# Holding back a kernel's second load until VectorE has built the identity matrix

## The chip, the cores and the metric

The kernel runs on one core of one Trainium2 chip. The metric is the time of one execution in microseconds (us) on the device, as the median of several executions. A second figure is used below, the *span*: the time from the first to the last instruction in the trace, which is about 1.8 us shorter than the time of the execution.

Some words are used throughout. An *issue* is the instruction with which SyncE starts a load. The load is then carried out by 16 DMA engines in pieces; the trace has one *record* for each piece, and a record of the first three loads is the 60 KB that go into one partition. A *descriptor* is the entry that tells a DMA engine to move one piece. A load has *landed* when its last record is in.

## The reference

```python
batch, seq, dim = 32, 512, 1024          # float32
def reference(x):
    return np.max(x, axis=-1).astype(np.float32)
```

16384 rows of 1024 numbers are reduced to 16384 maxima. 67.1 MB are read, 64 KB are written.

## The kernel before

The input goes through a ring of 46 rows in each of the 128 partitions. SyncE issues the loads, VectorE reduces each load with `reduce_max`. The first three loads have 15 rows each and fill 45 of the 46 places, so the fourth load cannot be issued until the first has been reduced. For a small part of the rows near the end TensorE, ScalarE and GpSimd take over a piece of the reduction, and for that VectorE builds an identity matrix at the start. The parts that matter here:

```python
    in_turn("DVE", nc.vector.memset(ident, 1.0))
    ...                                     # iota by scan, transpose, three small adds
    in_turn("DVE", nc.vector.tensor_scalar(
        out=ident, in0=colno, scalar1=rowno[:, 0:1], scalar2=None, op0=ALU.is_equal))
    ...
    for j in range(len(loads)):
        while issued < len(loads) and issued < j + 3:
            start, n, src, _ = loads[issued]
            held = any(s < start + n and start < s + k for s, k, _, _ in loads[j:issued])
            if held:                        # the place in the ring is still in use
                break
            nc.sync.dma_start(out=rows(issued), in_=src)
            issued += 1
        ...
            maximum(res[:, col:col + n - m], rows(j)[:, :n - m, :])
```

## Time and profile before

| | before |
|---|---|
| time, median of 5 | 164.09 us (163.90 to 164.27) |
| span of the profiled run | 162.3 us |
| share of the span in which the loads' queue is busy | 96.7% |
| VectorE busy | 135.4 us, 83% |
| issues of the first three loads | 0.72, 1.14, 1.62 us |
| VectorE ends the identity | 2.50 us |
| first reduction starts | 21.42 us |

The table is read like this. Two resources are near full, the 16 DMA engines and VectorE. About three quarters of VectorE's missing 17% (19.9 of 26.9 us) lie before the first reduction, because it has no data yet. The lines for this stand in the prediction.

### The profile page before, as it was taken

How to read it: one execution, taken by the hardware profiler on the slowest of the kernel's cores; microseconds unless marked ns; L12 is line 12 of the kernel's file. 1: busy time of each engine (PE TensorE's matmuls, PEld its weight loads, DVE VectorE, ACT ScalarE, POOL GpSimd, SP SyncE). 2: the span in 40 equal slices, each digit the busy share in tenths (PEclk: the TensorE clock that was granted, in tenths of full speed). 3: DMA queues.
4: the chain of work that ended last, by engine and by line, in shares of the span. 5: the costliest groups of instructions: out<-in, count | busy, mean ns of one | idle time of the engine just before them, and what ended most of it. 6: DMA issues, size and time to landing. Idle time of an engine off the chain costs nothing.

```text
span 162.3 us, 305 instructions
## 1 busy us (share of the span) xinstructions
PE 14.0 (9%) x76; PEld 12.0 (7%) x76; DVE 135.4 (83%) x35; ACT 6.3 (4%) x8; POOL 16.2 (10%) x11
## 2 busy tenths in 40 slices
PE   0000000000000000000000000000003010736540
PEld 0000000000000000000000000000002010725440
DVE  3000079995999779998999999999999999999994
ACT  3000000000000000000000000000001000222020
POOL 0000000000000000000000000000000500095970
DMA  7999699988999699999998998999999999999990
GB/s 242 485 485 454 273 485 485 485 379 348 485 485 485 285 410 452 452 452 388 497 472 371 433 455 355 436 436 420 509 396 445 452 395 396 440 411 423 405 379 18
DMA packets 3200, 67.18 MB, mean 414 GB/s; under 512 B 640, under 2 KB 640, under 8 KB 1408
## 3 DMA queue, kind: packets, MB, share of 16 engines
q1 hardware_dynamic: 2880, 67.11, 96.7%
q10 hardware_dynamic: 320, 0.07, 0.2%
HBM read 67.11 MB, written 0.07 MB: 414 GB/s over the span
## 4 chain that ended last, share of the span: by engine, by line
DVE 57%; DMA 36%; issue 5%; DVEq 0%
DVE res L168 52%; DMA ring<-in_x_dram 36%; DVE fetched L168 5%; DVEq L249 0%
## 5 line engine op out<-in xcount | busy, mean ns | idle before, releaser
L168 DVE TENSOR_REDUCE res<-ring 128x15 f32<-128x15360 f32 (+10 forms) x15 | 124.1, 8302 | 23.7 <-DMA ring<-in_x_dram 23.7
L143 POOL PARTITION_ALL_REDUCE top<-sb x7 | 16.0, 2330 | 141.8 <-ACT sb L141 141.8
L135 PE MATMUL ps<-ident,ring 128*128 128x128 f32 x38 | 9.3, 425 | 133.8 <-DMA ring<-in_x_dram 133.8
L135 PEld LDWEIGHTS ps<-ident,ring 128*128 128x128 f32 x38 | 7.5, 223 | 134.1 <-issue 127.8
L141 ACT COPY sb<-ps 128x768 f32<-128x768 f32 (+3 forms) x7 | 5.1, 739 | 150.2 <-PE ps L135 150.2
L168 DVE TENSOR_REDUCE fetched<-ring 128x2 f32<-128x1280 f32 (+3 forms) x5 | 8.5, 1699 | 0.0
L161 PE MATMUL fetched<-ident,top 1*128 1x1 f32 x38 | 4.8, 243 | 10.8 <-DVE fetched L168 7.3
L161 PEld LDWEIGHTS fetched<-ident,top 1*128 1x128 f32 x38 | 4.5, 213 | 12.5 <-issue 8.0
L168 DVE TENSOR_REDUCE res<-res 128x2 f32<-128x672 f32 (+1 forms) x2 | 1.7, 858 | 0.0
L141 ACT ACT_TABLE_LOAD x1 | 1.3, 1283 | 0.7 <-PEq L238 0.7
L83 DVE MEMSET ident<- 128x128 f32 x1 | 0.2, 165 | 0.8 <-PEq L238 0.8
L168 DVE TENSOR_REDUCE res<-fetched 128x2 f32<-128x8 f32 (+3 forms) x5 | 0.7, 158 | 0.0
L90 DVE TENSOR_SCALAR rowno<-rowno 32x1 f32<-32x1 f32 x3 | 0.4, 146 | 0.1
L85 DVE TENSOR_TENSOR_SCAN colno<-ident 128x128 f32<-128x128 f32 x1 | 0.4, 425 | 0.0
L92 DVE TENSOR_SCALAR ident<-colno,rowno 128x128 f32<-128x128 f32 x1 | 0.3, 285 | 0.0
L87 DVE STREAM_TRANSPOSE rowno<-colno 128x32 f32<-128x32 f32 x1 | 0.2, 213 | 0.0
L238 POOL MEMSET const-float32-0.0<- 128x1 f32 x1 | 0.1, 98 | 0.2 <-issue 0.2
L238 POOL MEMSET const-bfloat16-1.0<- 128x1 bf16 x1 | 0.1, 101 | 0.0
L238 POOL MEMSET const-uint8-127<- 128x1 uint8 x1 | 0.1, 101 | 0.0
L238 POOL MEMSET const-float32-1.0<- 128x1 f32 x1 | 0.1, 99 | 0.0
L84 DVE MEMSET rowno<- 128x32 f32 x1 | 0.1, 85 | 0.0
## 6 DMA issues: line engine op xcount, KB each, us to landing
ring<-in_x_dram SPq DMA_DIRECT2D x3, 7680.0 KB, 38.4
ring<-in_x_dram SPq DMA_DIRECT2D x1, 7168.0 KB, 37.0
ring<-in_x_dram SPq DMA_DIRECT2D x1, 6144.0 KB, 33.4
ring<-in_x_dram SPq DMA_DIRECT2D x1, 5632.0 KB, 28.6
ring<-in_x_dram SPq DMA_DIRECT2D x1, 4608.0 KB, 39.1
ring<-in_x_dram SPq DMA_DIRECT2D x1, 4096.0 KB, 33.3
ring<-in_x_dram SPq DMA_DIRECT2D x1, 3584.0 KB, 29.0
ring<-in_x_dram SPq DMA_DIRECT2D x1, 3072.0 KB, 35.9
```

What stands on the lines that cost most here:

```text
L83: in_turn("DVE", nc.vector.memset(ident, 1.0))
L84: in_turn("DVE", nc.vector.memset(rowno, 0.0))
L85: in_turn("DVE", nc.vector.tensor_tensor_scan(out=colno, data0=ident, data1=ident, initial=-1.0, op0=ALU.add, op1=ALU.mult))
L87: in_turn("DVE", nc.vector.transpose(out=rowno, in_=colno[:, :32]))
L90: in_turn("DVE", nc.vector.tensor_scalar(out=part, in0=part, scalar1=float(q * 32), scalar2=None, op0=ALU.add))
L92: in_turn("DVE", nc.vector.tensor_scalar(out=ident, in0=colno, scalar1=rowno[:, 0:1], scalar2=None, op0=ALU.is_equal))
L135: in_turn("PE", nc.tensor.transpose(out=ps[:, k * P:(k + 1) * P], in_=rows(j)[:, loads[j][1] - m + r + i, c0 * P:(c0 + 1) * P], identity=i ...
L141: in_turn("ACT", nc.scalar.copy(out=sb[:, :W], in_=ps[:, :W]))
L143: in_turn("POOL", nc.gpsimd.partition_all_reduce(top[:, :W], sb[:, :W], P, bass_isa.ReduceOp.max))
L161: in_turn("PE", nc.tensor.transpose(out=share(j)[:, c0, r + i:r + i + 1], in_=tops[j, c][0:1, k * P:(k + 1) * P], identity=ident[0:1, 0:1],))
L168: return in_turn("DVE", nc.vector.reduce_max(out=out, in_=in_, axis=X))
L238: nc = _bacc.Bacc("TRN2", target_bir_lowering=False, num_devices=1)
```

## The change

The intent, by the reason that the new line gives, is "first load alone": nothing else is to be issued while the first load starts.

```diff
-    in_turn("DVE", nc.vector.tensor_scalar(
+    ready = in_turn("DVE", nc.vector.tensor_scalar(
         out=ident, in0=colno, scalar1=rowno[:, 0:1], scalar2=None, op0=ALU.is_equal))
 ...
-            nc.sync.dma_start(out=rows(issued), in_=src)
+            load = nc.sync.dma_start(out=rows(issued), in_=src)
+            if issued == 1:
+                tc.add_manual_dep(load.ins, ready.ins.name, SYNC, reason="first load alone")
             issued += 1
```

## The prediction

> **What bounds the kernel now.** I read the page first (busy shares, then the DMA row of the forty slices), then the chain that ended last in order of time, then the waits of VectorE and of the loads' queue, then the first three microseconds of the timeline, and last the single DMA records of the trace.
>
> The page's busy line and DMA rows say that two things are nearly full, VectorE at 83% and the 16 DMA engines from the first slice to the last but one:
>
> ```profile
> PE 14.0 (9%) x76; PEld 12.0 (7%) x76; DVE 135.4 (83%) x35; ACT 6.3 (4%) x8; POOL 16.2 (10%) x11
> DMA  7999699988999699999998998999999999999990
> q1 hardware_dynamic: 2880, 67.11, 96.7%
> ```
>
> The loads' queue (q1) is busy for 96.7% of the 162.3 us span, 156.9 us. The dips to 6 in the slices are an effect of how long records are put into slices: each record of a large load covers one row group of 60 KB and takes 2.27 us, and in the records each engine takes the next one up in the same moment that it ends the last, with nothing longer than 0.06 us between, apart from single records that the trace seems to lack. 67.11 MB over 16 engines at 61440 bytes in 2.267 us (27.1 GB/s each, 434 together) is 154.8 us. The transfers begin at 1.72 us and end near 158.5 us, so their own start, about 155 us of data and a couple of microseconds of small losses are the whole span.
>
> The chain in order of time says the same for the first half, and shows where VectorE takes over:
>
> ```profile
> 0.66 0.07 issue
> 0.72 20.67 DMA ring<-in_x_dram
> 21.39 0.02 issue
> 21.42 16.16 DVE res L168
> 37.58 0.02 issue
> 37.60 37.02 DMA ring<-in_x_dram
> 74.62 0.02 issue
> 74.64 55.86 DVE res L168 x5
> ```
>
> The reader should see that the 37.02 us of the fourth load, issued at 37.60, are not its own transfer (7.34 MB at 434 GB/s is 16.9 us): it lies behind the third load in the queue. So up to 74.62 the clock is the stream of data, whatever the chain names. After 74.64 VectorE's reductions run end to end (the only other idle time it has is before that):
>
> ```profile
> DVE res L168 <- DMA ring<-in_x_dram: 23.7, 4, 18.9
> ```
>
> Those four waits are 18.91 us before the first reduction, 1.98 and 1.99 before the next two, 0.79 before the fourth. Hence everything later hangs on when the fourth load lands, and that on when the stream started and how fast it went.
>
> The start itself:
>
> ```profile
> 0.72 1.32 SPq L185 DMA_DIRECT2D ring<-in_x_dram  x3
> 0.82 0.17 DVE L83 MEMSET ident<- 128x128 f32 x1 [0.82 <-PEq L238]
> 0.94 0.09 DVE L84 MEMSET rowno<- 128x32 f32 x1
> 1.02 0.42 DVE L85 TENSOR_TENSOR_SCAN colno<-ident 128x128 f32<-128x128 f32 x1
> 1.48 0.21 DVE L87 STREAM_TRANSPOSE rowno<-colno 128x32 f32<-128x32 f32 x1
> 1.72 0.46 DVE L90 TENSOR_SCALAR rowno<-rowno 32x1 f32<-32x1 f32 x3
> 2.22 0.28 DVE L92 TENSOR_SCALAR ident<-colno,rowno 128x128 f32<-128x128 f32 x1
> ```
>
> Three loads are issued from 0.72 to 2.04 us: in single records the first takes 372 ns, the second starts at 1.14 and takes 425, the third starts at 1.62 and takes 424. VectorE finishes the identity at 2.22 + 0.28 = 2.50 us.
>
> **What the Trainium skill says.** "DMA: Bandwidth & Descriptors", section "Queues, rings and completion order", says that on each engine descriptors are consumed in ring order. The trace agrees: all sixteen engines do eight 2.27 us records of the first load before any of the second (the second load's first records start at 20.5 us). So the second load does not share bandwidth with the first now, and a "first load alone" gets no bandwidth back that way. The page "Perfetto Trace Analysis", section "DMA Instruction — HWDGE (DVE, Sync)", says the recorded span of an issue is the wait for and use of the descriptor generator, not the movement of data, and that an engine may begin while descriptors are still being made. The trace agrees: issues of 0.33 to 0.45 us stand for transfers of 16 us. "VectorE: DVE Perf Modes", section "The perf-mode tier table (the rule you actually need)", has tensor_reduce at 1x only; 15360 elements in 16.15 us is 0.951 elements per ns, so the reductions have no slack that a change in load timing could reach.
>
> **The change part by part.**
>
> Added: one wait on the second issue. It moves from 1.14 to about 2.50 + 0.05 = 2.55 us (0.05 from the 0.04 to 0.07 us between other VectorE ends and the dependent step in this timeline), the third from 1.62 to about 3.03 us. Late by 1.4 us, and it costs nothing: the engines need the second load's descriptors only when the first load's are used up, at 20.5 us, 17.5 us after the third issue. No instruction is removed, and the order on every engine stays the same; the built kernels show that only SyncE gets a split issue and a wait. The first load, the activation table and VectorE's steps are untouched.
>
> What could be gained lies in the first records. The sixteen first ones start between 1.72 and 2.52 us and take 3.0 us where they start early, against 2.267 us for every later one; the two that start last (2.44 and 2.52) take 2.27 and 2.33. All end together, between 4.68 and 4.94, but for one engine at 5.20. It is as if nothing moved at full speed before about 2.45 us, 1.7 us after the issue. That is when the third issue is through (2.04) plus some delay, so the descriptors of the second and third loads may be holding up the rest of the first load's. If so:
> - if the early starters lose their stretch but the last still starts at 2.52, the first round ends at 4.85 instead of 5.20: gain 0.35 us;
> - if all start with their neighbours, the slowest (start 2.02, took 3.17) ends at 2.02 + 2.27 = 4.29: gain 0.9 us;
> - if the stretch is a cold start that has nothing to do with the other issues: gain 0.
>
> Against the first two: the issue at 37.60, made in mid-stream, lengthened the records then in flight by at most 0.01 us (2.267 to 2.279). One more issue costs the engines almost nothing once they run. So I give no effect about half, and the gains the other half at some 0.55 us on average: -0.3 us.
>
> A gain at the start is passed on in full. The first landing moves the first reduction, which frees the slot for the fourth load; the stream is continuous, so landings two to four move as much; VectorE from 74.64 on has no idle time, and its later loads' issues hang on its own ends, so they move along too. Sum: 163.97 - 0.3 = 163.65 us.
>
> **The rivals.**
> 1. *Nothing at all.* The wait is hidden behind 17.5 us of queued data and the slow first records are a cold start. For it: the small cost of issues in mid-stream. It makes 163.9 to 164.0.
> 2. *The whole start-up stretch goes.* For it: the second and third issues take 425 ns where a lone one takes 328, so issues do crowd each other, and the end of the stretch falls just after the third. It makes 163.1, or 162.9 if the last engine also stops trailing the rest by 0.25 us, which it does through the first four landings.
> 3. *The late issue makes a hole in the stream.* It would need the first load's data to run out by 3 us; they last to 20.5. Against it the whole timeline; it would make more than 164 only if the queue behaved in another way than ring order.
> 4. *The engines' order shifts.* The stagger of the sixteen engines is set in the first round and kept for the whole kernel; another stagger may put one engine later, as one now is by 0.25 us. That is worth 0.2 us either way.
>
> **Range and chances.** The three runs of before lie within 163.9 and 164.27, so noise is 0.2 us. The largest plausible gain is 0.9 us, the largest plausible loss the stagger and noise, 0.4 us. The range is 163.0 to 164.2. A 2% change is 3.3 us, over three times the largest gain that I can build from the records and far over any loss; both sides get 1%.
>
> **What would show it.** In the changed profile, the second and third issues should stand at about 2.55 and 3.0 us; the sixteen first records should take about 2.3 to 2.7 us if the crowding is real, or still end at 4.7 to 5.2 us if not; the first reduction should start at 21.42 minus the gain (20.5 to 21.4), the fourth at 74.64 minus the same, and the time from the fourth to the end should not move. The second reduction's wait should stay at 1.98 us. I would be wrong if the first reduction moved one way and the end another, if VectorE waited for the second load by more than 2.2 us, or if the end moved by over 1 us: then something later in the stream depends on the early issues in a way that these views do not show.

## More of the kernel before

One view that it does not show is what SyncE, the issuer of the loads, waits for. In these lines of the kernel before, the columns are the waiting line, what it waited for, the total in us, how often, and the longest:

```profile
SPq L185 <- DVE res L168: 86.3, 6, 16.2
SPq L185 <- DMA ring<-in_x_dram: 37.6, 5, 19.4
...
SPq L238 <- PEq L238: 0.7, 1, 0.7
```

SyncE spends most of the kernel waiting, and the longest single wait is the 19.4 us from the third issue to the landing of the first load.

## The result, and the profile after

The changed kernel took 164.11 us (median of 5, 163.97 to 164.18), the kernel before 164.09 us (median of 5, 163.90 to 164.27). The ratio is 1.0003, with a 95% interval of 0.9991 to 1.0015. Ratios here are the mean time of one kernel's fast runs over that of the other's of the same rounds, so they are not quite the ratio of the medians quoted. The result is: no change.

The wait did go where it was meant to go. The first line below is from the timeline of the first microseconds of the changed kernel (start, duration, engine, instruction, count), the second the end of the identity:

```profile
0.72 2.63 SPq L185 DMA_DIRECT2D ring<-in_x_dram  x3
2.22 0.29 DVE L92 TENSOR_SCALAR ident<-colno,rowno 128x128 f32<-128x128 f32 x1
```

Three issues that took from 0.72 to 2.04 us now take until 3.35 us; the second stands at 2.54 and the third at 2.92. In the view of what SyncE waits for, with the columns as above, the new wait has a line of its own, and another line has shrunk:

```profile
SPq L185 <- DVE res L168: 86.3, 6, 16.2
SPq L185 <- DMA ring<-in_x_dram: 36.2, 5, 18.0
...
SPq L185 <- DVE ident L92: 1.4, 1, 1.4
```

The wait is 1.4 us long. The wait that follows it on the same engine, for the first landing, went from 19.4 to 18.0 us: the same 1.4 us less. This is what an absorbed wait looks like in a profile. It is not gone, it is taken out of a longer wait behind it.

The busy shares and the DMA rows of the page:

```profile
PE 14.0 (9%) x76; PEld 12.0 (7%) x76; DVE 135.4 (83%) x35; ACT 6.3 (4%) x8; POOL 16.2 (10%) x11
DMA  7997999979999599999998998999999999999991
q1 hardware_dynamic: 2880, 67.11, 96.8%
```

The chain that ended last, its first eight pieces (start, duration, what), and VectorE's waits for loads:

```profile
0.66 0.07 issue
0.72 20.62 DMA ring<-in_x_dram
21.34 0.02 issue
21.37 16.16 DVE res L168
37.53 0.02 issue
37.55 37.00 DMA ring<-in_x_dram
74.55 0.02 issue
74.57 55.86 DVE res L168 x5
```

```profile
DVE res L168 <- DMA ring<-in_x_dram: 23.6, 4, 18.9
```

The first reduction starts at 21.37 us in place of 21.42, the fourth at 74.57 in place of 74.64. These shifts of 0.05 and 0.07 us are a little larger than those between two executions of the changed kernel (21.37 and 21.39, then 74.57 and 74.61), and well under the 0.2 us of noise that the prediction allowed. From the fourth reduction's start to the end of the span it is 87.7 us in both kernels, and VectorE's waits are the same four. The second reduction, before and then after:

```profile
39.55 16.15 DVE L168 TENSOR_REDUCE res<-ring 128x15 f32<-128x15360 f32 x1 [1.98 <-DMA ring<-in_x_dram]
39.48 16.15 DVE L168 TENSOR_REDUCE res<-ring 128x15 f32<-128x15360 f32 x1 [1.96 <-DMA ring<-in_x_dram]
```

The figure in brackets is the idle time before it. The prediction wanted this wait to stay at 1.98 us.

### The profile page after: what moved, and what is told of

Its sections match the earlier page's. It is cut to its first block, busy times and chain, and to the rows that moved or that the text cites. A ratio compares the mean times of both kernels' runs of the same rounds, so it can differ in the third digit from the quotient of the medians.

```text
span 162.2 us, 305 instructions
## 1 busy us (share of the span) xinstructions
PE 14.0 (9%) x76; PEld 12.0 (7%) x76; DVE 135.4 (83%) x35; ACT 6.3 (4%) x8; POOL 16.2 (10%) x11
## 4 chain that ended last, share of the span: by engine, by line
DVE 57%; DMA 36%; issue 5%; DVEq 0%
DVE res L168 52%; DMA ring<-in_x_dram 36%; DVE fetched L168 5%; DVEq L251 0%
```

## The experiments

The result alone leaves something open. The prediction gave even chances to a gain of 0.35 to 0.9 us, which would come from first DMA records that are no longer slowed by the second and third issues. The measured zero can mean that there was no such slowing, or that the second issue, now at 2.54 us, slows the same records at another moment. I also wanted to see how much later the second issue may come, and whether a shift of the start reaches the end at all.

The table shows the sixteen first records of a stream of transfers, as the trace of each run has them. The kept trace doesn't name the engine of a record; that there is one for each engine is inferred from the order of starts and ends. A record of this size takes 2.267 us in mid-stream. Each run is told below.

```
                issues of the loads    first records start   mean length   they end
before          0.72, 1.14, 1.62       1.72 to 2.52          2.89 us       4.68 to 5.20
changed         0.72, 2.54, 2.92       1.72 to 2.63          3.03          4.71 to 5.14
after_again     0.72, 2.54, 2.92       1.72 to 2.42          2.98          4.71 to 5.17
late_10         0.73, 12.68, 13.06     1.73 to 2.52          2.94          4.57 to 5.05
first_waits     2.53, 2.95, 3.43       3.54 to 4.30          2.93          6.37 to 6.90
landed, load 2  21.38 (load 3: 21.76)  22.35 to 22.97        2.97          25.18 to 25.77
```

### after_again: the changed kernel once more

No edit.

> The changed kernel once more, unedited, five rounds. Theory A (the wait is hidden behind the 17 us of the first load's data, and the slow first records are a cold start): ratio to the kernel before 0.999 to 1.001, the first reduction starting within 0.1 us of 21.4 us, sixteen first records of about 2.3 to 3.3 us again. Theory B (the descriptors of the second load do slow the first records, a gain of 0.3 us that noise covered): ratio 0.998, first reduction at 21.1 us or before.

Measured: 164.06 us (median of 5) against 164.04 us; ratio 1.000, interval 0.9988 to 1.0013. The first reduction starts at 21.39 us. These are theory A's numbers, and theory B's hidden gain of 0.3 us (0.2%) is outside the interval. That the slow records are a cold start, this run doesn't test.

### late_10: the same wait, ten microseconds longer

```diff
+    for _ in range(6):
+        ready = in_turn("DVE", nc.vector.memset(res, 0.0))
```

These lines stand after the identity in the changed kernel. The area that is cleared is written again later, and the results are correct.

> The wait of the change, only longer: six clears of a scratch area follow the identity on VectorE, and the second load waits for the last, at an estimated 8 to 12 us. Theory A: 164.0 us, no change, because the first load's data last to 20.5 us; its sixteen first records still take about 3 us. Theory B (in the changed kernel the second issue, at 2.54 us, merely falls on the first records at another point and slows them as much): now nothing is issued while they run, so they take 2.27 us, the first reduction starts 0.35 to 0.9 us before 21.4, and the time is 163.1 to 163.6 us. Theory C (a late second issue costs as it stands): longer by up to the delay, 5 to 10 us.

Measured: 164.02 us (median of 4) against 164.04 us; ratio 0.9998, interval 0.9985 to 1.0012. The issues of the first three loads, and the first reduction:

```profile
0.73 12.75 SPq L187 DMA_DIRECT2D ring<-in_x_dram  x3
21.36 16.15 DVE L170 TENSOR_REDUCE res<-ring 128x15 f32<-128x15360 f32 x1 [8.71 <-DMA ring<-in_x_dram]
```

The second issue stands at 12.68 us, over 7 us after the last first record has ended, and the first records are as slow as ever: 2.94 us on average. So theory B falls. The descriptors of other loads are not what slows the first records, since here there were none. Whether the making of the first load's own descriptors does, this run leaves open. Theory C falls too: eleven and a half microseconds of delay cost nothing.

### landed: the second load waits until the first is there

```diff
-            nc.sync.dma_start(out=rows(issued), in_=src)
+            load = in_turn("SP", nc.sync.dma_start(out=rows(issued), in_=src))
+            if issued == 0:
+                lead = load
             if issued == 1:
-                tc.add_manual_dep(load.ins, ready.ins.name, SYNC, reason="first load alone")
+                tc.add_manual_dep(load.ins, lead.ins.name, SYNC, reason="first load landed")
```

The edit is to the changed kernel. The loads at the end are put into the same order on SyncE, so that no later load can be moved ahead of the one that waits.

> The second load waits until the first has landed, so it is issued at about 21.4 us, after the data have run out at 20.5 to 21.0 us. Theory A: a hole in the stream from 20.8 us to the second load's first record, 1.0 us after the issue, so about 22.4 us: landings two to four and the end later by 1.6 us, 165.6 us, and by 2.3 us, 166.3 us, if the engines' first records after the hole are again 0.7 us too long. Rival (VectorE idles about 2 us before the second and third reductions, so there is slack): under 0.3 us.

Measured: 166.57 us (median of 4) against 164.04 us, 2.5 us longer; ratio 1.0153, interval 1.0139 to 1.0167. The timeline (start, duration, what, then in brackets the idle time before and what ended it) of VectorE, and after the dots the fourth reduction of the kernel before:

```profile
21.39 16.15 DVE L168 TENSOR_REDUCE res<-ring 128x15 f32<-128x15360 f32 x1 [18.88 <-DMA ring<-in_x_dram]
41.97 16.15 DVE L168 TENSOR_REDUCE res<-ring 128x15 f32<-128x15360 f32 x1 [4.42 <-DMA ring<-in_x_dram]
60.11 16.16 DVE L168 TENSOR_REDUCE res<-ring 128x15 f32<-128x15360 f32 x1 [1.99 <-DMA ring<-in_x_dram]
77.06 15.09 DVE L168 TENSOR_REDUCE res<-ring 128x14 f32<-128x14336 f32 x1 [0.80 <-DMA ring<-in_x_dram]
...
74.64 15.09 DVE L168 TENSOR_REDUCE res<-ring 128x14 f32<-128x14336 f32 x1 [0.79 <-DMA ring<-in_x_dram]
```

The wait before the second reduction grew from 1.98 to 4.42 us, by 2.44 us, and it is not made good anywhere: the fourth reduction starts at 77.06 in place of 74.64 us, and the execution takes 2.5 us longer. Idle time of VectorE in front of a load is no slack if the stream of data is what sets the end. The loss has the two parts expected. The engines stand still from 20.5 to 21.0 us, when each runs out, to 22.35 to 22.97 us, about 1.8 us; and their first records after the pause are again 0.7 us too long, at a time when nothing of the kernel's launch is left. So the slow start comes with starting the stream, and not with the start of the program.

### first_waits: the wait on the first load instead

```diff
-            if issued == 1:
+            if issued == 0:
                 tc.add_manual_dep(load.ins, ready.ins.name, SYNC, reason="first load alone")
```

As in landed, the order of SyncE's loads is fixed.

> The wait for the identity is put on the first load instead of the second, so the first issue moves from 0.72 to about 2.54 us. Theory A with a cold start that belongs to the issue: first records from 3.54 us, again about 3 us long, everything later by 1.82 us, 165.8 us. Theory D (the engines can't move data at full speed before about 2.45 us after the program's start, whatever is issued): the first records take 2.27 us, and all is later by 1.0 to 1.1 us, 165.1 us. Rival E (a shift of the start is not passed on to the end): under 0.3 us.

Measured: 165.78 us (median of 4) against 164.04 us, 1.74 us longer; ratio 1.0106, interval 1.009 to 1.0121. The fourth reduction in the timeline:

```profile
76.34 15.09 DVE L168 TENSOR_REDUCE res<-ring 128x14 f32<-128x14336 f32 x1 [0.78 <-DMA ring<-in_x_dram]
```

The first issue moved from 0.72 to 2.53 us, 1.81 us; the fourth reduction moved by 1.70 and the end by 1.74 us. A shift of the stream's start reaches the end nearly whole, so rival E falls. The first records are slow again, though they start 1.8 us later, so theory D, a stall until 2.45 us after the program's start, falls as well.

### late_18 and late_19: how late is too late

Both are late_10 with nine and with ten clears instead of six.

> As late_10 with nine clears instead of six; the last one should end near 17.8 us, so the second load is issued at about 17.8 us and its first record can start 1.0 us later, at 18.8, before the first load's data run out at 20.5. Theory A (only an issue less than 1.0 us before the data run out costs anything): no change, 164.0 us, second reduction's wait 2.0 us as before. Rival (the engines take new records in only some microseconds ahead, or the queue needs two loads' worth ahead): longer by 0.5 us or more.

> As late_10 with ten clears; the last should end near 19.5 us, so the second issue stands about 1.0 us before the data run out at 20.5 us. Theory A: right at the edge; the engines that start their share of the second load late (0.3 to 0.8 us after the first of them) get a hole and a slow first record, so the time is 164.0 plus 0.1 to 0.8 us. Rival as in late_18: plus 1.5 us or more.

Measured, late_18: the second issue stands at 17.79 us. The time is 164.49 us (median of 4) against 163.98 us; ratio 1.0027, interval 1.0012 to 1.0042. That contradicts the expected 164.0, but the trace shows nothing late. The same lines as above, of late_18:

```profile
21.33 16.15 DVE L170 TENSOR_REDUCE res<-ring 128x15 f32<-128x15360 f32 x1 [3.57 <-DMA ring<-in_x_dram]
39.37 16.15 DVE L170 TENSOR_REDUCE res<-ring 128x15 f32<-128x15360 f32 x1 [1.88 <-DMA ring<-in_x_dram]
57.51 16.16 DVE L170 TENSOR_REDUCE res<-ring 128x15 f32<-128x15360 f32 x1 [2.00 <-DMA ring<-in_x_dram]
74.46 15.09 DVE L170 TENSOR_REDUCE res<-ring 128x14 f32<-128x14336 f32 x1 [0.79 <-DMA ring<-in_x_dram]
```

The second reduction waits 1.88 us, not more than before, and the spans of the four executions are 162.1 to 162.4 us, like those of the kernel before. What grew is the time outside the span: time less span is 2.15 to 2.22 us in all four, against 1.74 to 1.83 in the executions of before. This needed a control, which follows.

Measured, late_19: the second issue stands at 19.51 us, 1.0 us before the data run out. The time is 164.93 us (median of 4) against 163.98 us, 0.95 us longer, a little over the 0.1 to 0.8 expected; ratio 1.0052, interval 1.0035 to 1.0068. Here time less span is the usual 1.75 to 1.83 us, and the span itself grew to between 162.8 and 163.3. All sixteen first records of the second load are slow (2.42 to 2.99 us), and the second reduction waits 2.50 us. I had put the edge at the time from issue to first record, 1.0 us, but an issue that comes just then still meets the slow start on every engine, though the engines had hardly stood still (their records of the first load end between 20.37 and 20.93 us, and the new ones start between 20.47 and 21.16). The lead that counts seems to be that to full flow, some 1.7 us (1.0 to the first record and 0.7 by which it is too long). From 20.4 us, where the first engine runs out, this gives an estimate of 18.7 us for the last harmless issue. The runs show only that it lies between 17.79 and 19.51 us.

### clears_only and late_18_again: the control

clears_only is the kernel before with nine clears on VectorE and no added wait; late_18_again is late_18 unedited.

```diff
+    for _ in range(9):
+        in_turn("DVE", nc.vector.memset(res, 0.0))
```

> Control for late_18, whose launches took 0.4 us longer while their spans stayed at 162.1 to 162.4 us: the same nine clears on VectorE, but the second load doesn't wait for them, as in the kernel before. If the 0.4 us belongs to the program with its nine clears and lies outside the span: again 164.4 to 164.6 us with spans of 162.1 to 162.4. If it belongs to the late issue: 164.0 us.

> late_18 unedited, beside its control on the same chip. If the 0.4 us is a property of the program: 164.4 to 164.6 us again, spans 162.1 to 162.4. If it was a chance of one sitting: 164.0 us.

Measured: clears_only 164.44 us (median of 4), late_18_again 164.52 us (median of 4), before 163.97 us; ratios 1.0035 (1.0015 to 1.0054) and 1.0031 (1.0014 to 1.0047). In both, time less span is 2.15 to 2.24 us in every execution. So the 0.4 us belongs to the program with nine clears, with or without the late issue, and lies outside the span. The wait of late_18 costs nothing. Why nine clears add time there, and six (1.73 to 1.79 us in late_10) or ten do not, these runs do not show.

### split_first: a first load of small records

```diff
-            nc.sync.dma_start(out=rows(issued), in_=src)
+            if issued == 0:
+                nc.sync.dma_start(out=rows(0)[:, :1, :], in_=src[:, :1, :])
+                nc.sync.dma_start(out=rows(0)[:, 1:, :], in_=src[:, 1:, :])
+            else:
+                nc.sync.dma_start(out=rows(issued), in_=src)
```

> The kernel before with the first load issued in two parts: one row of each partition (4 KB records), then the other fourteen (56 KB). If the slow start is a fixed delay of some 0.7 us until data flow, whatever the size of the record: the first 4 KB records take 0.15 + 0.7 us, the first reduction starts at 21.4 us plus up to 0.3 us (eight more records per engine), the time stays within 0.3 us of 164.0. If it is in proportion to the record (3.0 for 2.27): the 4 KB records take about 0.2 us and the start is shorter by 0.6 us, 163.4 us.

Measured: 164.11 us (median of 4) against 163.98 us; ratio 1.0004, interval 0.999 to 1.0019. The first 4 KB records take 0.39 to 1.09 us, 0.77 on average, where such a record takes 0.16 us in mid-stream; the first reduction starts at 21.41 us. So the slow start adds about 0.6 us to a record of 4 KB and about 0.7 us to one of 60 KB: a delay that hardly depends on the size, and that smaller records don't shorten.

### split_parts and split_halves: a first load of fewer partitions

```diff
-            nc.sync.dma_start(out=rows(issued), in_=src)
+            if issued == 0:
+                nc.sync.dma_start(out=rows(0)[:16], in_=src[:16])     # split_halves: 64
+                nc.sync.dma_start(out=rows(0)[16:], in_=src[16:])     # split_halves: 64
+            else:
+                nc.sync.dma_start(out=rows(issued), in_=src)
```

> The kernel before with the first load issued in two parts: 16 partitions (one record for each engine), then the other 112. If the slow start is the time to make the descriptors of a 128-partition load, a sixteenth-size first issue lets the engines start together and unstretched, the first reduction starts 0.4 to 0.8 us earlier and the time is 163.2 to 163.6 us. If it is a fixed delay between the issue and the flow of data: first records still end near 4.7 to 5.2 us, 164.0 us within 0.2.

> The first load issued as partitions 0 to 63 and then 64 to 127. In split_parts a load of 16 partitions and one of 112 ran at well under full rate (records of 8.1 and 4.4 to 5.4 us in place of 2.27). If that is because a load reaches only the memory ports of its own partitions[...], each half runs at half rate, its records take about 4.5 us, the first load 36 us in place of 18, and the time is 164.0 + 18 = 182 us. If it came of the odd sizes (16 and 112) or of two issues for one load: records of 2.27 us and 164.0 us, within 0.5.

Measured: split_parts took 184.54 us (median of 4) against 163.98 us, ratio 1.1256 (1.1237 to 1.1275), and missed both of its expectations by 20 us. Its first sixteen records take 8.1 us on average, 3.6 times the usual. I had overlooked what the Trainium skill says on the page "SBUF — State Buffer", section "Door 1: The DMA port swizzle (why `[64,N]` ≈ `[32,N]`)": that the bandwidth of a DMA follows from how many of the 16 ports its partitions reach, 4 ports for partitions 0 to 15, 8 for partitions 0 to 63. split_halves was made to test that. It took 184.17 us (median of 2) against 163.97 us, ratio 1.1227 (1.1205 to 1.125). Three stretches of it (interval; its length; busy time and count of PE, PEld, DVE, ACT and POOL; clock; DMA share; GB/s):

```profile
1.70:10.00 8.30, 0.00 (x0) 0.00 (x0) 0.72 (x4) 0.30 (x1) 0.00 (x0) 1.00 1.13 237
10.00:40.00 30.00, 0.00 (x0) 0.00 (x0) 0.00 (x0) 0.00 (x0) 0.00 (x0) 1.00 1.00 213
42.00:58.00 16.00, 0.00 (x0) 0.00 (x0) 15.79 (x1) 0.00 (x0) 0.00 (x0) 1.00 0.99 430
```

From 10 to 40 us the halves move at 213 GB/s with all engines busy; the loads of 128 partitions behind them move at 430. The length of the records gives 205 and 434 GB/s (16 engines, 61440 bytes in 4.80 and in 2.267 us); such a window is less exact, since it is not a whole number of records. Records of 4.80 in place of 2.27 us, eight on each engine, are 20.2 us more, and the first reduction starts at 41.63, 20.2 us later. The time is 2.2 us above the 182 expected, because the records are a little longer than the 4.5 us assumed. This agrees with the page: half of the ports, and a little less than half of the rate. Two issues for one load are not the reason, since split_first has them too and took 164.11 us. That the 112 partitions of split_parts collide on ports in the same way is likely, but was only argued.

So the slow start was not tested by these two kernels: the long records cover it.

## Why the prediction was right, point by point

**The bound.** The prediction took the stream of data as what sets the time up to the fourth landing, and VectorE, without a gap, from there on. first_waits (1.81 us at the issue, 1.74 at the end) and landed (2.44 us at the second reduction, 2.5 at the end) show it: a shift of the stream arrives almost whole.

**The added wait costs nothing.** It was put at 1.4 us late with 17.5 us to spare. It measured 1.4 us, and came out of the following wait. late_10 used over 11 us of the spare time at no cost and late_18 over 16; the reserve ended between 17.79 and 19.51 us.

**The gain in the first records.** This term was mis-sized. The sum had -0.3 us, from even chances of a gain of some 0.55 us, and the failed step is "the descriptors of the second and third loads may be holding up the rest of the first load's". The runs showed in its place rival 1, a cold start: with the next issue at 2.54 or at 12.68 us the first records were just as slow (3.03 and 2.94 us on average, 2.89 before), and they were slow again after the pause in landed. That in the kernel before the slow start ended shortly after the third issue was a coincidence. The prediction's own evidence, that an issue in mid-stream lengthened records by 0.01 us at most, was the better guide and deserved more weight than half.

**The stagger of the engines.** The last engine trails by less in the changed kernel (its first record ends at 5.14 us, not 5.20). That is about the shift of 0.05 us at the first reduction, well under the 0.2 us allowed.

**Range and chances.** 164.11 us lies within 163.0 to 164.2, near its upper end, as it must if the gain is zero. There was some luck in that: one execution of the kernel before took 164.27 us, above the range, so a true zero could have fallen outside. The mean forecast, 163.65 us, was 0.46 us too low, most of it the gain that did not come. That the outcome would be within 2% followed from the largest gain that the prediction could build, 0.9 us.

**Small errors in the working.** None of them moves the result. A load of 7.86 MB at 434 GB/s takes 18.1 us, not the "transfers of 16 us". The first of an engine's eight records took 2.27 to 3.17 us, not 2.27. 163.97 - 0.3 is 163.67, and the middle of 0.35 and 0.9 is 0.63, not 0.55. Rival 2's 162.9 counts the trailing engine twice, since the gain of 0.9 us already takes that engine's end from 5.20 to 4.29 us. And that an engine may begin while descriptors are still being made is not seen here: the first issue ends at 1.09 us and the first record starts at 1.72.

What stays open is why a stream's first records are about 0.7 us too long (the first load's own descriptors are a rival that no run tested), and the 0.4 us outside the span with nine clears. None of the kernels beats the kernel before.

## What to carry to other kernels

Before working out what a delayed issue costs, look at how much data is still queued ahead of it: if the first load occupies the engines for 18 us, the second may come 11.5 us late at no cost, and coming early buys nothing either. Where the stream of data sets the end, never let it run dry: in landed, the issue after the pause took 1.0 us to the first record and another 0.7 us until full flow. And read an absorbed wait by its neighbour: the new line in the waits is matched by an equal loss in the wait behind it.

## What the Trainium skill lacked or had wrong

- "DMA: Bandwidth & Descriptors", section "Latency and other measured facts", gives about 600 ns to the first byte for a DMA issued from SyncE. It does not say from where it counts. Here the first records start 1.0 us after the start of the issue (0.72 to 1.72 us; 21.38 to 22.35 us in landed), which is 0.63 to 0.64 us after its end and so agrees if the end is meant. The page doesn't say that the first records are then about 0.7 us too long, so that full flow is reached some 1.7 us after the issue's start, nor that this comes back after a pause of under 2 us. (It has a least round trip to memory of a similar size, but for tiny transfers and not for the start of a stream.)
- The same page, section "Rules for kernel authors", says of two transfers to disjoint partition halves not to bother, because they serialize on the same engines. Serializing alone need not cost anything; the halves ran at about 205 GB/s in place of 434 and cost 20.2 us for one load of 7.86 MB. The halved rate follows from the ports on "SBUF — State Buffer", but this rule does not say it.
- I found no page that would explain why a program with nine more VectorE clears takes 0.4 us longer outside its span (2.15 to 2.24 in place of 1.74 to 1.83 us), while six or ten more do not.
